# Building a product-key expert layer's gates once, with its activations written out and read back

## The chip, the cores and the metric

The kernel runs on one core of a Trainium2 chip, in one launch. The metric is the time on the device in microseconds (us); the time given for a kernel is the median of its runs.

## What is computed

Two model blocks run on 256 tokens of 1024 features. The change touches one part of the first block, a layer of 128 x 128 = 16384 single-neuron experts from which eight heads choose sixteen each for every token. The chosen pairs of keys come from two searches, and the rest is dense in the kernel: an activation for every expert and token, times a gate that is zero for what was not chosen.

```python
v1, i1 = lax.top_k(s1, PEER_TOPK)            # s1, s2: scores against 128 first and 128 second keys
v2, i2 = lax.top_k(s2, PEER_TOPK)
cand = (v1[..., :, None] + v2[..., None, :]).reshape(T, PEER_HEADS, PEER_TOPK * PEER_TOPK)
vals, ci = lax.top_k(cand, PEER_TOPK)
idx = jnp.take_along_axis(i1, ia, axis=-1) * PEER_NKEYS + jnp.take_along_axis(i2, ib, axis=-1)
gates = jax.nn.softmax(vals, axis=-1)
# for each block of tokens
u = expert_u[ii]
h = jnp.einsum('tkd,td->tk', u, xx).astype(f32)
a = (jax.nn.gelu(h) * gg).astype(x.dtype)
out = jnp.einsum('tk,tkd->td', a, expert_v[ii])
```

## The kernel before, in words

All large products take weights in units of 128 x 1024 fp32. `Emit.run` (L85) walks a list of items in program order; a "w" item is the product of one unit, an "e" item other work. A unit is loaded on SyncE's queue (L96) and split in two parts: ScalarE casts the first, `whi` (L106), VectorE makes the second, `wlo` = raw - whi (L107). There are three buffers of each part, so the split of unit k+3 is written into unit k's buffers. Its instructions are issued right after the product of unit k, and the cast waits until TensorE is through with that product. What an evacuation needs (`em.later`) is issued behind the split.

An expert unit b holds the 128 experts of first key b (the second key is the partition). The layer has two stages of 128 units each:

- **Input products** (`expert_u0`, `expert_e`): 24 matmuls of 128x256 (three for each of 8 chunks, L243 to L245) into one of the four PSUM banks `wk`, which are taken in turn; then GELU on ScalarE. Units 0 to 63 leave their activations in the tile `G0` (128 x 64 x 256 fp32), units 64 to 127 in pairs in DRAM (`uD`, written by GpSimd's queue, L1276). The searches run on VectorE beside units 0 to 63.
- **Output products** (`expert_v`): each unit multiplies one activation, split into `ah` and `al` two units ahead (L374, L375), into four banks `acc` that stay for all 128 units.

The gates are built in groups of 8 tokens by `gbuild(half, g)`, 32 groups for each half of the first keys. `one_hot` makes four tiles on VectorE: `p1` (which pair has which first key, 64 keys), `p2` (the same for the 128 second keys), `ph` and `p1` again (times the high and the low part of the gate). `place` multiplies them on TensorE, 16 matmuls of 128x64 into one `wk` bank (L1248, L1249), which I call a block. For half 0 VectorE multiplies the bank onto `G0` (L1253), among input units 64 to 127; for half 1 ScalarE copies it to `G1` (L1256), among output units 0 to 60. Which unit each step stands before is a table:

```python
gb.setdefault(GB0 + g * GB1 // 31 + 2 * n, []).append(it)         # n = 0 one_hot, n = 1 place
places.setdefault((58 * g + 30) // 31 + 2 * n, []).append(it)
```

So a group's block stands two units behind its one-hots. The second half's activations are read back (L1359) and multiplied with `G1` (L1389, `gated`) in output units 64 to 127.

Of the kernel before, what the change touches and what calls it, by code (L numbers as in the profile page):

```python
# [20 lines left out]
P = 128  # L21
# [27 lines left out]
class Emit:  # L49
    """Items in program order; the weights that they take run ahead of them."""  # L50
# [85 lines left out]
class Halves:  # L136
    """[P, 8, T] in two tiles."""
# [46 lines left out]
def spread(a, b):  # L184
    """Both lists in their orders, evenly among one another."""
# [11 lines left out]
def body(ctx, tc, I, out):  # L197
# [24 lines left out]
    def table(func):  # L222
        """has the engine load a function's table before it is needed."""
# [14 lines left out]
    uD = dram.tile([P, 64, T], F32, name="uD")  # L238
# [21 lines left out]
    def qsum(qs):  # L260
        """four tiles added up, onto the first."""
# [35 lines left out]
    def parts_of(x, gain, y, wk, ready, then=None):  # L297
        """these steps after the last product: the weights' splits come between."""
# [8 lines left out]
    def mm3s(ps, sp, xh, xl, width):  # L307
        """units on the first parts, then on the second ones."""
# [10 lines left out]
    def late_norm(x, r, gain, n, of, when, shift=None, lag=1):  # L319
        """hi + lo = x * r * gain (+ shift) in steps, chunk d in of(d) from the when[d]-th weight item on, or all at once."""  # L320
# [18 lines left out]
    def shift_parts(c0, y):  # L339
        """a shift in two parts behind the tokens."""  # L340
# [9 lines left out]
    def unit_y(ap, y, evac, bank, width=T + 2):  # L350
        """a unit on a norm's input, with a shift's products behind the tokens'."""
# [11 lines left out]
    def npair(pl, tag, width=T):  # L363
        """the pair in npool has room for a shift behind the tokens."""
# [12 lines left out]
    def split_half(src, hi, lo):  # L377
        """of src / 2."""
# [3 lines left out]
    def chunks(o, hi, lo, x, width, order=range(KD)):  # L382
        """a unit's product, chunk of rows by chunk of rows."""
# [6 lines left out]
    def fm(ap, x, evac, bank=bankB):  # L390
        """128 output features on partitions."""
# [6 lines left out]
    def tm(aps, xs, evac, bank):  # L398
        """512 output columns, tokens on partitions; one bank for each (x, token tile)."""
# [24 lines left out]
    class Acc:  # L424
        """1024 output features on partitions, over any number of rows of weights."""
# [16 lines left out]
    def gate_y(pa_, pb_, wk):  # L442
        """in steps: r (x + shift's) of both halves, and silu of the first times the second."""
# [13 lines left out]
    def ffn(w13, w2, y, nx, wk, done, rest, early, ctx=None, mc=None):  # L457
        """items; done(acc) after the last. y holds the norm's input times its gain, and its shift behind the tokens,
        for the first units; rest follows the very first ones and leaves E_["r"], and the norm in nx for the units from
        the early ones on. With ctx, the context's norm: nx holds it behind the tokens, and its activations are left in  # L460
        mc(j)."""
# [11 lines left out]
        def gate(j):  # L473
# [29 lines left out]
            # once the product two before it is through  # L503
# [68 lines left out]
        # the last activations have one product more before they are needed  # L572
# [4 lines left out]
    # ======================= block 1 ========================================  # L577
# [10 lines left out]
    # products of no use keep the array's clock from its idle rate until the first weights are there  # L588
# [3 lines left out]
    # silu(c) of x and the context, on every partition  # L592
# [10 lines left out]
    # constants  # L603
# [4 lines left out]
    # key number, for each of 4 tokens  # L608
# [112 lines left out]
    def decay_logs():  # L721
        """the same of the decays, begun."""
# [4 lines left out]
    def gla_z():  # L727
        # log_sigmoid(z) = min(z, 0) - ln(1 + exp(-|z|))
# [86 lines left out]
    def gla_n():  # L815
        """1/rms of each head's outputs, tokens on partitions: a column for each (head, token tile)."""
# [15 lines left out]
    def gla_r(p):  # L832
        """the same on all partitions: the sums over a diagonal."""
# [99 lines left out]
    # branches: a unit holds two groups of 128 columns, each with 4 chunks of rows  # L933
# [53 lines left out]
    # the branches' steps before these units  # L987
# [10 lines left out]
    # modulation: rows of w_ada^T against silu(c), one output for each partition  # L998
# [20 lines left out]
    # ======================= experts =========================================  # L1019
# [11 lines left out]
    def open_b():  # L1031
        A.close()
        g0 = Gx.enter_context(tc.tile_pool(name="g0", bufs=1))
        B["G", 0] = g0.tile([P, 64, T], F32, name="G0")
        pb = Bx.enter_context(tc.tile_pool(name="pb", bufs=1))
        B["p"] = pb
# [9 lines left out]
    def ctx_norm(name, c0, x, qs, n):  # L1046
        """the context's norm, in steps; x is lost."""
# [40 lines left out]
    def top16(which, width):  # L1088
        """of each (row, values, places), in turn."""
# [17 lines left out]
    # pair (a, b) of a side's ranks comes after all (a' <= a, b' <= b), so (a + 1)(b + 1) <= 16 for a chosen one:  # L1107
    # a = 0 with 16 b, a = 1..3 with 8, a = 4..7 with 4, a = 8..15 with 1, in the order of 16 a + b
# [18 lines left out]
    def pick(t, s_):  # L1127
        """the key that each chosen pair has on side s_, in steps."""
        def a():
# [5 lines left out]
            if s_ == 0:  # L1135
                # a = the number of starts up to the place, less 1: the sum of the keys' steps over them
# [5 lines left out]
            else:  # L1142
                # b = the place & 15, 7, 3, 0 in the four parts
# [30 lines left out]
    def gates(t):  # L1174
        """softmax over each head's pairs, split in two halves; keys and gates to [pair, token]."""
# [41 lines left out]
    def gbuild(half, g):  # L1217
        """gates of all pairs of keys for NG tokens, first keys of one half: [key 2, key 1, token],
        the first half's onto its experts' activations."""
# [3 lines left out]
        def one_hot():  # L1223
            pb = B["pg"]

            def of(t, n):
                """[P, 2, n, 4] of [P, 8]."""
                return t[:, ts].rearrange("p (g t) -> p g t", g=2).unsqueeze(2).to_broadcast([P, 2, n, 4])

            def keys(lo, n):  # L1230
                return iota[:, lo:lo + n, :].unsqueeze(1).to_broadcast([P, 2, n, 4])

            p1 = pb.tile([P, 2, 64, 4], F16, name="p1", tag="p1", bufs=2)
            dve.tensor_tensor(out=p1, in0=keys(half * 64, 64), in1=of(i1T, 64), op=ALU.is_equal)
            p2 = pb.tile([P, 2, P, 4], F16, name="p2", tag="p2", bufs=2)
            dve.tensor_tensor(out=p2, in0=keys(0, P), in1=of(i2T, P), op=ALU.is_equal)
            ph = pb.tile([P, 2, 64, 4], F16, name="ph", tag="ph", bufs=2)
            dve.tensor_tensor(out=ph, in0=p1, in1=of(ghT, 64), op=ALU.mult)
            dve.tensor_tensor(out=p1, in0=p1, in1=of(glT, 64), op=ALU.mult)
            box["t"] = (p2, p1, ph)  # L1240

        def place():
            p2, p1, ph = box.pop("t")
# [6 lines left out]
            ps3 = ps.rearrange("p (t i) -> p t i", t=NG)  # L1250
            o3 = B["G", half][:, :, ts].rearrange("p i t -> p t i")
            if half == 0:
                em.later(lambda: dve.scalar_tensor_tensor(out=o3, in0=ps3, scalar=1.0 / GSCALE, in1=o3,  # L1253
                                                          op0=ALU.mult, op1=ALU.mult))
            else:
# [4 lines left out]
    def open_pg():  # L1260
        B["pg"] = B["p"]
# [854 lines left out]
```

## Time and profile before

| | |
|---|---|
| median of 3 runs (lowest, highest) | 2036.58 us (2035.91, 2038.29) |
| span of the profiled execution | 2036.1 us |
| TensorE matmuls, busy | 2021.8 us (99%) |
| VectorE / ScalarE / GpSimd busy | 1449.1 / 988.5 / 83.9 us |
| chain that ended last, TensorE's share | 94% |

The span reaches from the first instruction to the last. A matmul's record covers its whole passage, and records of neighbours overlap: what one costs is read from the distance between starts in the timeline. Releasers of waits are inferred from semaphores.

### The profile page before, as it was taken

The page shows a single profiled execution, that of the slowest core. Times are in us where ns is not written, and L with a number is a line of the kernel's source. Part 1 is how long each engine was busy: PE and PEld are TensorE (multiplying, and loading weights), DVE is VectorE, ACT ScalarE, POOL GpSimd, SP SyncE. Part 2 cuts the span into 40 slices and gives each one's busy share as a digit, 9 for nine tenths or more (in the row PEclk, how much of TensorE's full clock was granted, in tenths as well). Part 3 has the DMA queues.
Part 4 walks back from the last instruction along what each step waited for, and adds up shares of the span by engine and source line. Part 5 has one row for each costly group of instructions (what it writes and reads, how often), then busy time and mean ns, then how long its engine had stood idle before and what let it go on. Part 6 is the DMA issues. An engine that isn't in the chain of part 4 may idle for free.

```text
span 2036.1 us, 38555 instructions
## 1 busy us (share of the span) xinstructions
PE 2021.8 (99%) x15860; PEld 1941.8 (95%) x15860; DVE 1449.1 (71%) x2410; ACT 988.5 (49%) x1478; POOL 83.9 (4%) x168
## 2 busy tenths in 40 slices
PE   9999999999999999999999999999999999999998
PEld 8899999999999999999998888899989999999998
DVE  7668788877887777789876777578655565568655
ACT  6555545443334555644564333244744455446444
POOL 0000000000000000011000000001000000000000
PEclk9999999999999999999999999999999999999999
DMA  6646555566556556588673666668543333455653
GB/s 243 199 158 192 170 183 182 182 192 194 196 192 209 168 181 197 163 271 280 214 249 115 197 197 205 199 218 297 185 133 106 113 114 112 148 171 174 187 187 124
DMA packets 103952, 376.44 MB, mean 185 GB/s; under 512 B 12055, under 2 KB 12439, under 8 KB 103392
## 3 DMA queue, kind: packets, MB, share of 16 engines
q1 hardware_dynamic: 85968, 310.55, 48.0%
q0 software_dynamic: 16800, 60.74, 9.0%
q8 instruction: 124, 2.03, 0.4%
q10 hardware_dynamic: 1008, 2.70, 0.3%
q14 instruction: 52, 0.43, 0.1%
HBM read 363.45 MB, written 10.49 MB: 184 GB/s over the span
## 4 chain that ended last, share of the span: by engine, by line
PE 94%; DVE 2%; DMA 2%; ACT 1%; issue 0%; SPq 0%; DVEq 0%; ACTq 0%; POOLq 0%
PE wk L243 18%; PE wk L245 18%; PE wk L244 18%; PE acc L243 10%; PE acc L244 10%; PE acc L245 10%; PE acc L414 2%; PE acc L415 2%; PE acc L416 2%; PE wk L1248 2%; PE wk L1249 2%; DVE wlo L107 1%; DMA raw<-pv_dram 1%; DMA raw<-w_dram 1%; ACT whi L106 1%; PE acc L1080 0%
## 5 line engine op out<-in xcount | busy, mean ns | idle before, releaser
L107 DVE TENSOR_TENSOR wlo<-raw,whi 128x1024 fp32r<-128x1024 f32 x587 | 717.3, 1224 | 478.0 <-ACT whi L106 476.2
L106 ACT CAST whi<-raw 128x1024 fp32r<-128x1024 f32 x587 | 615.4, 1049 | 752.8 <-PE wk L244 401.6
L243 PE MATMUL wk<-nhi,whi 128*128 128x256 f32 (+1 forms) x1744 | 495.0, 284 | 0.0
L245 PE MATMUL wk<-nhi,wlo 128*128 128x256 f32 (+1 forms) x1744 | 491.8, 282 | 0.3 <-DVE wlo L107 0.3
L244 PE MATMUL wk<-nlo,whi 128*128 128x256 f32 (+1 forms) x1744 | 490.1, 281 | 0.0
L243 PE MATMUL acc<-ah,whi 128*128 128x256 f32 x1376 | 390.4, 284 | 0.0
L244 PE MATMUL acc<-al,whi 128*128 128x256 f32 x1376 | 388.3, 282 | 0.6 <-DVE al L375 0.4
L245 PE MATMUL acc<-ah,wlo 128*128 128x256 f32 x1376 | 388.1, 282 | 0.0
L244 PEld LDWEIGHTS wk<-nlo,whi 128*128 128x128 f32 x1744 | 329.6, 189 | 0.6 <-issue 0.5
L245 PEld LDWEIGHTS wk<-nhi,wlo 128*128 128x128 f32 x1744 | 329.6, 189 | 0.5 <-DVE wlo L107 0.5
L243 PEld LDWEIGHTS wk<-nhi,whi 128*128 128x128 f32 x1744 | 329.1, 189 | 0.9 <-issue 0.5
L244 PEld LDWEIGHTS acc<-al,whi 128*128 128x128 f32 x1376 | 259.4, 188 | 2.0 <-DVE al L375 1.2
L243 PEld LDWEIGHTS acc<-ah,whi 128*128 128x128 f32 x1376 | 260.1, 189 | 0.9
L245 PEld LDWEIGHTS acc<-ah,wlo 128*128 128x128 f32 x1376 | 259.4, 189 | 0.0
L244 PE MATMUL wk<-nxl,whi 128*128 128x512 f32 (+1 forms) x544 | 188.5, 346 | 0.0
L243 PE MATMUL wk<-nxh,whi 128*128 128x512 f32 (+1 forms) x544 | 188.2, 346 | 0.0
L245 PE MATMUL wk<-nxh,wlo 128*128 128x512 f32 (+1 forms) x544 | 187.4, 344 | 0.0
L374 ACT CAST ah<-G 128x256 fp32r<-128x256 f32 x128 | 52.2, 408 | 177.6 <-PE acc L245 169.6
L245 PEld LDWEIGHTS wk<-nxh,wlo 128*128 128x128 f32 x544 | 102.2, 188 | 13.2
L243 PEld LDWEIGHTS wk<-nxh,whi 128*128 128x128 f32 x544 | 102.1, 188 | 13.0
L244 PEld LDWEIGHTS wk<-nxl,whi 128*128 128x128 f32 x544 | 102.1, 188 | 11.8
L375 DVE TENSOR_TENSOR al<-G,ah 128x256 fp32r<-128x256 f32 x128 | 54.2, 423 | 33.4 <-ACT ah L374 33.1
(536 smaller groups left out, 3312.5 us busy)
## 6 DMA issues: line engine op xcount, KB each, us to landing
raw<-pu_dram SPq DMA_DIRECT2D x128, 512.0 KB, 3.5
raw<-pv_dram SPq DMA_DIRECT2D x128, 512.0 KB, 4.2
row<-ada_dram POOLq DMA_DIRECT2D x59, 512.0 KB, 4.6
raw<-f13a_dram SPq DMA_DIRECT2D x44, 512.0 KB, 3.6
raw<-f2a_dram SPq DMA_DIRECT2D x44, 512.0 KB, 4.5
raw<-f13b_dram SPq DMA_DIRECT2D x44, 512.0 KB, 3.6
raw<-w_dram SPq DMA_DIRECT2D x41, 512.0 KB, 4.2
raw<-f2b_dram SPq DMA_DIRECT2D x22, 512.0 KB, 3.6
```

Source lines behind the costliest of these rows:

```text
L106: nc.scalar.copy(hi, r)
L107: nc.vector.tensor_tensor(out=lo, in0=r, in1=hi, op=ALU.subtract)
L243: pe.matmul(o, whi, xhi, start=start, stop=False)
L244: pe.matmul(o, whi, xlo, start=False, stop=False)
L245: pe.matmul(o, wlo, xhi, start=False, stop=stop)
L374: act.copy(hi, src)
L375: dve.tensor_tensor(out=lo, in0=src, in1=hi, op=ALU.subtract)
L414: pe.matmul(o, xh[:, k, ts], hi[:, sl], start=k == 0, stop=False)
L415: pe.matmul(o, xh[:, k, ts], lo[:, sl], start=False, stop=False)
L416: pe.matmul(o, xl[:, k, ts], hi[:, sl], start=False, stop=k == KD - 1)
L1248: pe.matmul(o, p2[:, g4, :, t4], ph[:, g4, :, t4], start=True, stop=False)
L1249: pe.matmul(o, p2[:, g4, :, t4], p1[:, g4, :, t4], start=False, stop=True)
```

## The change

`gbuild(g)` builds the gates for all 128 first keys at once, in 32 groups. All four tiles have 128 keys x 8 tokens (1024 elements). `place(0)` and `place(1)` take four tokens each: 8 matmuls of 128x128 into a bank of their own, which ScalarE copies to one tile `G` (128 x 128 x 256 fp32). The three steps stand before three consecutive units, all among input units. Every unit's activation goes to DRAM by itself (128 writes of 128 KB in place of 32 of 256 KB; two buffers `act`), and all are read back in pairs (64 reads in place of 32, six ahead after the first), multiplied with `G` (L1384 in the new numbering) and split. The output products have no gate building left. Comments are gone too, so line numbers shift by 2 to 16.

```diff
-TKE, GB0, GB1 = 64, 66, 59
+TKE, GB0, GB1 = 63, 64, 58
+NE = 7
...
-    uD = dram.tile([P, 64, T], F32, name="uD")
+    uD = dram.tile([P, P, T], F32, name="uD")
...
-            p1 = pb.tile([P, 2, 64, 4], F16, name="p1", tag="p1", bufs=2)
-            dve.tensor_tensor(out=p1, in0=keys(half * 64, 64), in1=of(i1T, 64), op=ALU.is_equal)
+            keys = iota.unsqueeze(1).to_broadcast([P, 2, P, 4])
+            p1 = pb.tile([P, 2, P, 4], F16, name="p1", tag="p1", bufs=2)
+            dve.tensor_tensor(out=p1, in0=keys, in1=of(i1T), op=ALU.is_equal)
             p2 = pb.tile([P, 2, P, 4], F16, name="p2", tag="p2", bufs=2)
-            dve.tensor_tensor(out=p2, in0=keys(0, P), in1=of(i2T, P), op=ALU.is_equal)
-            ph = pb.tile([P, 2, 64, 4], F16, name="ph", tag="ph", bufs=2)
-            dve.tensor_tensor(out=ph, in0=p1, in1=of(ghT, 64), op=ALU.mult)
-            dve.tensor_tensor(out=p1, in0=p1, in1=of(glT, 64), op=ALU.mult)
+            dve.tensor_tensor(out=p2, in0=keys, in1=of(i2T), op=ALU.is_equal)
+            ph = pb.tile([P, 2, P, 4], F16, name="ph", tag="ph", bufs=2)
+            dve.tensor_tensor(out=ph, in0=p1, in1=of(ghT), op=ALU.mult)
+            dve.tensor_tensor(out=p1, in0=p1, in1=of(glT), op=ALU.mult)
...
-        def place():
-            p2, p1, ph = box.pop("t")
+        def place(g4):
+            p2, p1, ph = box["t"]
             ps = bankB()
-            for i in range(NG):
-                o = ps[:, i * 64:i * 64 + 64]
-                g4, t4 = i // 4, i % 4
+            for t4 in range(4):
+                o = ps[:, t4 * P:t4 * P + P]
                 pe.matmul(o, p2[:, g4, :, t4], ph[:, g4, :, t4], start=True, stop=False)
                 pe.matmul(o, p2[:, g4, :, t4], p1[:, g4, :, t4], start=False, stop=True)
...
+            em.later(lambda: act.activation(out=o3, in_=ps3, func=AF.Copy, scale=1.0 / GSCALE))
+
+        return ("e", None, one_hot), ("e", None, lambda: place(0)), ("e", None, lambda: place(1))
...
+            u = B["pu"].tile([P, T], F32, name="act", tag="act", bufs=2)
+            act.activation(out=u, in_=ps[:, :T], func=AF.Gelu_apprx_tanh)
+            pool.dma_start(out=uD[:, b, :], in_=u)
...
-        for n, it in enumerate(gbuild(0, g)):
-            gb.setdefault(GB0 + g * GB1 // 31 + 2 * n, []).append(it)
...
+        for n, it in enumerate(gbuild(g)):
+            gb.setdefault(GB0 + g * GB1 // 31 + 1 + n, []).append(it)
+    gb[GB0] = [E(em.flush), E(lambda: open_g())]
+    gb.setdefault(GB0 + GB1 - 4, []).append(E(lambda: load_early(0)))
+    gb[GB0 + GB1 + 3] += [E(em.flush), E(lambda: open_e()), E(lambda: gated(0))]
+    gb[GB0 + GB1 + 4] = [E(lambda: ready1(0)), E(em.flush)]
+    gb[GB0 + GB1 + 5] = [E(lambda: ready1(1))]
...
+    def open_e():
+
+        Cgx.close()
+        B["pe"] = Gx.enter_context(tc.tile_pool(name="pear", bufs=NE - 1))
+        for n in range(1, NE):
+            load_early(n)
...
     def ready1(b):
-        n = b // 2 - 32
+        n = b // 2
         ready(b, C["e", n][:, b % 2, :])
         if b % 2 == 0:
             em.later(lambda: gated(n + 1))
-        elif n + 8 < 32:
-            load_early(n + 8)
+        elif 0 < n and n + NE - 1 < 64:
+            load_early(n + NE - 1)
...
-        for n, it in enumerate(gbuild(1, g)):
-            places.setdefault((58 * g + 30) // 31 + 2 * n, []).append(it)
-    places[60].append(E(lambda: em.later(lambda: gated(0))))
```

How the order moves, at three places. Numbers behind a name tell tiles apart; `whi_5515` and `wlo_5516` are the two parts of one unit.

VectorE and TensorE among the input products, kernel before, around the one-hots `p2_5540`. Each TensorE row stands for a whole unit (24 matmuls) or a whole block (16).

```order
L107 TENSOR_TENSOR wlo_5516<-raw_5513,whi_5515 128x1024
L1234 TENSOR_TENSOR p1_5538<-iota_126,i1T_179 128x512
L1236 TENSOR_TENSOR p2_5540<-iota_126,i2T_180 128x1024
L1238 TENSOR_TENSOR ph_5542<-p1_5538,ghT_181 128x512
L1239 TENSOR_TENSOR p1_5538<-p1_5538,glT_182 128x512
L107 TENSOR_TENSOR wlo_5573<-raw_5570,whi_5572 128x1024
```

```order
L243 MATMUL wk_5488<-nhi_2300,whi_5373 128x256
L1248 MATMUL wk_5521<-ph_5451,p2_5449 128x64
L243 MATMUL wk_5545<-nhi_2300,whi_5423 128x256
L243 MATMUL wk_5579<-nhi_2300,whi_5481 128x256
L1248 MATMUL wk_5612<-ph_5542,p2_5540 128x64
L243 MATMUL wk_5636<-nhi_2300,whi_5515 128x256
```

The one-hots stand on VectorE behind `wlo_5516`, whose unit takes the buffers of the unit `whi_5373`. From the end of that unit to the block that needs `p2_5540`, TensorE has one block and two units.

The same two engines and the same place in the changed kernel, around the one-hots `p2_5748` (blocks of 8 matmuls).

```order
L109 TENSOR_TENSOR wlo_5730<-raw_5727,whi_5729 128x1024
L1231 TENSOR_TENSOR p1_5746<-iota_126,i1T_179 128x1024
L1233 TENSOR_TENSOR p2_5748<-iota_126,i2T_180 128x1024
L1235 TENSOR_TENSOR ph_5750<-p1_5746,ghT_181 128x1024
L1236 TENSOR_TENSOR p1_5746<-p1_5746,glT_182 128x1024
L109 TENSOR_TENSOR wlo_5781<-raw_5778,whi_5780 128x1024
```

```order
L245 MATMUL wk_5702<-nhi_2300,whi_5590 128x256
L1244 MATMUL wk_5737<-ph_5655,p2_5653 128x128
L245 MATMUL wk_5753<-nhi_2300,whi_5634 128x256
L1244 MATMUL wk_5788<-ph_5750,p2_5748 128x128
L245 MATMUL wk_5797<-nhi_2300,whi_5685 128x256
L1244 MATMUL wk_5832<-ph_5750,p2_5748 128x128
L245 MATMUL wk_5848<-nhi_2300,whi_5729 128x256
```

Here `wlo_5730` takes the buffers of the unit `whi_5590`. From the end of that unit to the first block that needs `p2_5748`, TensorE has one half block and one unit.

TensorE and ScalarE in the changed kernel where two groups follow each other without a free unit, which happens four times: `g * 58 // 31` then grows by 1 and not by 2. `G_5359` is the tile `G`, the banks are `wk`.

```order
L1244 MATMUL wk_6073<-ph_6035,p2_6033 128x128
L245 MATMUL wk_6089<-nhi_2300,whi_5970 128x256
L1244 MATMUL wk_6124<-ph_6035,p2_6033 128x128
L1244 MATMUL wk_6133<-ph_6086,p2_6084 128x128
L245 MATMUL wk_6142<-nhi_2300,whi_6014 128x256
L1244 MATMUL wk_6178<-ph_6086,p2_6084 128x128
L245 MATMUL wk_6194<-nhi_2300,whi_6065 128x256
```

```order
L108 CAST whi_6116<-raw_6114 128x1024
L1249 ACTIVATE G_5359<-wk_6073 128x4x128
L1257 ACTIVATE act_6121<-wk_6089 128x256
L108 CAST whi_6169<-raw_6167 128x1024
L1249 ACTIVATE G_5359<-wk_6124 128x4x128
L1249 ACTIVATE G_5359<-wk_6133 128x4x128
L1257 ACTIVATE act_6175<-wk_6142 128x256
```

With four banks in turn, the unit `wk_6142` takes the bank of `wk_6073`, and `wk_6194` that of `wk_6124`. Each of these is emptied behind a cast.

## Rows read from the trace of the kernel before

**Rows 1.** Page, the span and the engines' busy time.

```profile
span 2036.1 us, 38555 instructions
PE 2021.8 (99%) x15860; PEld 1941.8 (95%) x15860; DVE 1449.1 (71%) x2410; ACT 988.5 (49%) x1478; POOL 83.9 (4%) x168
```

**Rows 2.** Busy time by stage: input units 0-63, 64-127, output units 0-62.

```profile
core 0: us, PE busy (x) PEld busy (x) DVE busy (x) ACT busy (x) POOL busy (x), PEclk, DMA share, GB/s
250.00:433.00 183.00, 183.00 (x1543) 183.00 (x1543) 152.01 (x477) 90.62 (x136) 0.00 (x0) 1.00 0.59 183
440.00:647.80 207.80, 207.80 (x1974) 206.51 (x1974) 165.75 (x214) 82.04 (x124) 16.19 (x30) 1.00 0.60 195
647.80:860.80 213.00, 213.00 (x2023) 211.58 (x2022) 157.28 (x255) 121.31 (x161) 8.00 (x15) 1.00 0.58 182
```

**Rows 3.** Groups of instructions by line, 647.8 to 860.8 us (output units).

```profile
L1256 ACT ACTIVATE G<-wk 128x512 f32<-128x512 f32 x32 | 35.8, 1119 | 0.0
L1249 PE MATMUL wk<-p,p 128*128 128x64 f16 x256 | 35.3, 241 | 0.0
```

**Rows 4.** Timeline of TensorE, two units and two blocks, input units 64-127: start us, length.

```profile
526.16 0.28 PE L245 MATMUL wk<-nhi,wlo 128*128 128x256 f32 x1
526.28 0.23 PE L1248 MATMUL wk<-ph,p 128*128 128x64 f16 x1
...
532.92 0.28 PE L245 MATMUL wk<-nhi,wlo 128*128 128x256 f32 x1
533.04 0.23 PE L1248 MATMUL wk<-ph,p 128*128 128x64 f16 x1
...
533.95 0.24 PE L1249 MATMUL wk<-p,p 128*128 128x64 f16 x1
534.00 0.36 PE L243 MATMUL wk<-nhi,whi 128*128 128x256 f32 x1
534.20 0.28 PE L244 MATMUL wk<-nlo,whi 128*128 128x256 f32 x1
```

**Rows 5.** Timeline of TensorE, matmuls of 512 columns.

```profile
36.58 0.39 PE L415 MATMUL acc<-wlo,nhi 128*128 128x512 f32 x1
36.81 0.39 PE L416 MATMUL acc<-whi,nlo 128*128 128x512 f32 x1
```

**Rows 6.** Timelines of ScalarE and VectorE, the same two units as rows 4.

```profile
526.36 1.06 ACT L106 CAST whi<-raw 128x1024 fp32r<-128x1024 f32 x1 [1.52 <-PE wk L244]
527.32 0.39 ACT L1274 ACTIVATE scr<-wk 128x256 f32<-128x256 f32 x1
```

```profile
527.46 1.23 DVE L107 TENSOR_TENSOR wlo<-raw,whi 128x1024 fp32r<-128x1024 f32 x1 [0.36 <-ACT whi L106]
528.60 0.42 DVE L1234 TENSOR_TENSOR p<-iota,i1T 128x512 f16<-128x512 f16 x1
528.94 0.68 DVE L1236 TENSOR_TENSOR p<-iota,i2T 128x1024 f16<-128x1024 f16 x1
529.54 0.41 DVE L1238 TENSOR_TENSOR ph<-p,ghT 128x512 f16<-128x512 f16 x1
529.99 0.42 DVE L1239 TENSOR_TENSOR p<-p,glT 128x512 f16<-128x512 f16 x1
```

**Rows 7.** Waits of ScalarE and VectorE, 440 to 648 us: total us, times, longest.

```profile
ACT whi L106 <- PE wk L244: 124.5, 60, 2.6
...
DVE wlo L107 <- ACT whi L106: 40.5, 55, 2.7
```

**Rows 8.** DMA to and from `uD`: the products, and landing times of writes, then reads.

```profile
L1389 DVE TENSOR_TENSOR G<-G,G x32: 681/684/690, 861.1 to 1037.3; 128x512 f32<-128x512 f32 x32
```

```profile
DMA to landing us min/median/max: 2.3/2.5/5.1
```

```profile
DMA to landing us min/median/max: 2.8/4.6/8.0
```

**Rows 9.** TensorE's longest early wait, and the granted clock around it.

```profile
8.92 0.38 PE L919 MATMUL acc<-yah,whi 128*128 128x256 f32 x1 [1.34 <-ACT whi L106]
...
8.00:12.00 4.00, 3.02 (x21) 2.66 (x22) 3.55 (x8) 4.00 (x7) 0.00 (x0) 1.00 0.69 241
```

More of the change, by code (lines that the diff above doesn't have):

```diff
@@ L1032, in open_b @@
         A.close()
[L1033 to L1034 removed]
         pb = Bx.enter_context(tc.tile_pool(name="pb", bufs=1))
[L1036 removed]
+        B["p"] = B["pu"] = pb
         for s_ in range(2):
@@ L1215, in body, with gbuild @@
     NG = 8
-    def gbuild(half, g):
+    def gbuild(g):
         ts = slice(g * NG, g * NG + NG)
@@ L1223, in one_hot, with of @@
         def one_hot():
[L1224 to L1231, printed above, removed]
-            p1 = pb.tile([P, 2, 64, 4], F16, name="p1", tag="p1", bufs=2)
-            dve.tensor_tensor(out=p1, in0=keys(half * 64, 64), in1=of(i1T, 64), op=ALU.is_equal)
+            pb = B["p"]
+            def of(t):
+                return t[:, ts].rearrange("p (g t) -> p g t", g=2).unsqueeze(2).to_broadcast([P, 2, P, 4])
@@ L1252, in place @@
[L1252 to L1255, printed above, removed]
-                em.later(lambda: act.activation(out=o3, in_=ps3, func=AF.Copy, scale=1.0 / GSCALE))
-        return ("e", None, one_hot), ("e", None, place)
-    def open_pg():
-        B["pg"] = B["p"]
-    def expert_u0(b):
-        def ev(ps):
-            act.activation(out=B["G", 0][:, b, :], in_=ps[:, :T], func=AF.Gelu_apprx_tanh)
-        return fm(I["pu"][b], X2, ev)
@@ L1269, in expert_e @@
-    def expert_e(b):
-        def ev(ps):
-            if b % 2 == 0:
-                B["early"] = scr(B["p"], (P, 2, T))
-            act.activation(out=B["early"][:, b % 2, :], in_=ps[:, :T], func=AF.Gelu_apprx_tanh)
-            if b % 2 == 1:
-                pool.dma_start(out=uD[:, b - 65:b - 63, :], in_=B["early"])
+            ps3 = ps.rearrange("p (t i) -> p t i", t=4)
+            t0 = g * NG + 4 * g4
+            o3 = B["G"][:, :, t0:t0 + 4].rearrange("p i t -> p t i")
+            em.later(lambda: act.activation(out=o3, in_=ps3, func=AF.Copy, scale=1.0 / GSCALE))
@@ L1310, in body @@
     items += [("w", list(I["wq"][0:2]), first_units)] + [early_q(j) for j in range(2, NQ - 1)]
-    items += [("e", None, em.flush), ("e", None, open_b), ("e", None, open_pg), ("e", None, lambda: first_q(range(4)))]
+    items += [("e", None, em.flush), ("e", None, open_b), ("e", None, lambda: first_q(range(4)))]
     items += [early_q(NQ - 1), ("e", None, lambda: first_q([4]))]
@@ L1328, in body @@
         tk += pick(t, 0) + ga_[:1] + pick(t, 1) + ga_[1:]
-    ub = [expert_u0(b) for b in range(64)]
+    ub = [expert_u(b) for b in range(P)]
     ub[1:1] = [score(15)]
     ub[0:0] = [score(14)]
-    ub += [expert_e(b) for b in range(64, P)]
     gb = {}
     for g in range(T // NG):
-        for n, it in enumerate(gbuild(0, g)):
-            gb.setdefault(GB0 + g * GB1 // 31 + 2 * n, []).append(it)
-    for b in range(2):
-        gb[GB0 + GB1 + 3 + b] = [E(lambda b=b: ready(b, B["G", 0][:, b, :]))]
+        for n, it in enumerate(gbuild(g)):
[5 more added lines that the diff above has]
+    gb[GB0 + GB1 + 5] = [E(lambda: ready1(1))]
     items += over(ub, gb, TKE, tk)
@@ L1342, in body, with open_g @@
     Cgx = ExitStack()
-    def open_c():
+    def open_g():
         Bx.close()
-        g1 = Gx.enter_context(tc.tile_pool(name="g1", bufs=1))
-        B["G", 1] = g1.tile([P, 64, T], F32, name="G1")
-        B["pg"] = Cgx.enter_context(tc.tile_pool(name="pg", bufs=1))
+        g = Gx.enter_context(tc.tile_pool(name="g", bufs=1))
+        B["G"] = g.tile([P, P, T], F32, name="G")
+        B["pu"] = Gx.enter_context(tc.tile_pool(name="pu", bufs=1))
+        C["e", 0] = B["pu"].tile([P, 2, T], F32, name="early0")
+        B["p"] = Cgx.enter_context(tc.tile_pool(name="pg", bufs=1))
+    def open_e():
[3 more added lines that the diff above has]
+            load_early(n)
     def part(a, n):
-        return B["G", 0][:, a:a + n, :]
+        return B["G"][:, a:a + n, :]
     def flat(t):
@@ L1357, in load_early @@
     def load_early(n):
-        C["e", n] = part(2 * (n % 8), 2)
+        if n > 0:
+            C["e", n] = B["pe"].tile([P, 2, T], F32, name="early", tag="early")
         pool.dma_start(out=C["e", n], in_=uD[:, 2 * n:2 * n + 2, :])
@@ L1382, in ready1 @@
             em.later(lambda: gated(n + 1))
-        elif n + 8 < 32:
-            load_early(n + 8)
+        elif 0 < n and n + NE - 1 < 64:
+            load_early(n + NE - 1)
     def gated(n):
-        if n < 32:
-            dve.tensor_tensor(out=C["e", n], in0=C["e", n], in1=B["G", 1][:, 2 * n:2 * n + 2, :], op=ALU.mult)
+        if n < 64:
+            dve.tensor_tensor(out=C["e", n], in0=C["e", n], in1=part(2 * n, 2), op=ALU.mult)
     def expert_v(b):
@@ L1479, in body @@
     first = []
-    places = {}
-    for g in range(T // NG):
-        for n, it in enumerate(gbuild(1, g)):
-            places.setdefault((58 * g + 30) // 31 + 2 * n, []).append(it)
-    places[60].append(E(lambda: em.later(lambda: gated(0))))
-    loads = {36: lambda: load_early(0), 38: lambda: load_early(1), 40: lambda: load_early(2),
-             42: lambda: load_early(3), 44: lambda: load_cs(pool, 0), 46: lambda: load_cs(pool, 1), 48: lambda: load_early(4),
-             50: lambda: load_early(5), 52: lambda: load_ctx(0), 54: lambda: load_ctx(1), 55: silu_cs,
-             56: lambda: load_early(6), 58: lambda: load_early(7), 60: load_rows}
+    loads = {44: lambda: load_cs(pool, 0), 46: lambda: load_cs(pool, 1), 52: lambda: load_ctx(0),
+             54: lambda: load_ctx(1), 55: silu_cs, 60: load_rows}
     for b in range(64):
@@ L1492, in body @@
         first += [ev(b)]
-        first += places.get(b, [])
         if b in loads:
@@ L1506, in body @@
         lambda: em.later(lambda: ncc([0, 1, 2, 3, 4, 5, 6, 7])))]
-    items += [("e", None, open_c)] + first + [("e", None, Cgx.close)]
+    items += first
     for i, u in enumerate(second):
```

5 lines of the change are left out of this document (1 added, 4 removed).

## The prediction

> **What bounds the kernel now.** I read the page's busy times first, then the busy time by stage, then the timelines of a few units, then the waits. TensorE is busy for 99% of the 2036.1 us [rows 1], and in the three expert stages that the change touches it has no gap at all: 183.0 of 183.0, 207.8 of 207.8 and 213.0 of 213.0 us, at full clock [rows 2]. So every microsecond of matmul that goes there shortens the run, and every wait that appears there lengthens it. VectorE is busy for 80% of the middle stage and ScalarE for 39% [rows 2]; they have time left, but not at any moment: the cast of a unit's weights waits for TensorE to end the unit three before (60 waits, 124.5 us) and the second part waits for the cast (55 waits, 40.5 us) [rows 7]. VectorE takes its instructions in order, so whatever stands behind that second part on its queue starts only then.
>
> One unit and one block are priced by starts. From block to block there are two units: 526.28 to 533.04, 6.76 us. The block's sixteen matmuls start 0.061 us apart (533.04 to 533.95 is fifteen steps); from its first start to the second matmul of the next unit are 1.16 us, of which 0.12 is that unit's own first step (526.16 to 526.28) [rows 4]. So a block costs 1.04 us, 0.97 of it matmuls and 0.07 the change from one kind to the other, and a unit (6.76 - 1.04) / 2 = 2.86 us.
>
> **The change, part by part.**
>
> *Output products.* 32 blocks go, 512 matmuls in all (256 on each of two lines, [rows 3]): 32 x 1.04 = **-33.3 us**, all on the path, since TensorE is busy throughout. VectorE's one-hots and ScalarE's copies go there too, at no gain.
>
> *Input products, matmuls.* 32 blocks of sixteen 64-column matmuls become 64 half blocks of eight 128-column ones. No row shows a 128-column fp16 matmul. At 64 columns the step is 0.061 us; at 256 columns 0.12 [rows 4], and at 512 columns 0.23 [rows 5]. Those two differ by 0.11 for 256 columns, which led back to 128 columns gives 0.06 and at 64 would give 0.04: the 64-column step is already above the columns' own time. So I take 0.061, the end nearest to that line, and keep 0.118 as the other. A half block is 8 x 0.061 + 0.07 = 0.56 us; 64 x 0.56 - 33.3 = **+2.5 us**. The Trainium skill, "TensorE: Matmul & The Clock Gate", section "Back-to-back issue gap", gives about 81 ns as the sustained step of weight load and matmul at 128 columns; by it the sum below would be about 2059 us. The rows are nearer, so they stand.
>
> *Input products, the one-hots.* Now they have time to spare: the unit ends at 526.28 (where the block starts), the cast starts at 526.36, the second part at 527.46, the one-hots at 528.60, and the last ends at 529.99 + 0.42 = 530.41; the block wants them at 533.04 [rows 4, 6]. The margin is 2.63 us. The change takes from it three times. The first half block stands one unit sooner: 2.86. What stands ahead of the unit in between is half a block: 1.04 - 0.56 = 0.48. And the one-hots are longer: now 528.60 to 530.41, 1.81 us; then the two comparisons at 0.60 each (as 528.94 to 529.54), and the two dependent products at 0.45 and 0.42 [rows 6] plus 0.26 each for 512 elements more (0.68 - 0.42), 2.61 us in all: 0.80. The margin becomes 2.63 - 2.86 - 0.48 - 0.80 = -1.51 us. TensorE waits 1.5 us at a group's first half block. (The first of the eight matmuls needs only three of the tiles and goes ahead, 0.06; the signal takes about 0.08, as from 526.28 to 526.36. They cancel.) Nothing makes up for the wait: the next group's one-hots hang by the same chain on a unit that was itself late, so it recurs. While TensorE waits the other engines run dry too, so nothing is late behind them: second parts and casts have a whole unit to spare.
>
> The groups with this wait: of 32, the four that follow another without a free unit have their one-hots in time, and so has the group behind each (below). 24 x 1.5 = 36.0; the first of them has no half block ahead, 0.6 more: **+36.6 us**.
>
> *Input products, banks.* Units and half blocks alternate in four banks, so each bank comes round after two units, which ScalarE can meet: cast 1.06, copy 1.12, GELU 0.39 [rows 3, 6] are 2.6 of 3.4 us. At the four places with two half blocks in a row a unit comes round to a bank whose copy stands behind a cast that waits for the unit just ended: 0.08 + 1.06 + 1.12 = 2.26 us after it, against two half blocks of work (1.12), a wait of 1.15; and at the next unit 2.26 against one half block (0.56), 1.7. After that the next one-hots are in time. 4 x 2.85 = **+11.4 us**.
>
> *Writes and reads.* In input units each activation is written alone. The buffer is wanted again two units on, 5.7 us; GELU 0.39, some 0.3 to the issue and 2.5 us to land (5.1 at worst) [rows 6, 8] stay below or at it. SyncE's weight loads are untouched. The reads of output units 0 to 63 are new: 32 more, landing in 4.6 us (8.0 at worst) [rows 8], ordered six pairs ahead (twelve units, 34 us); VectorE's product of 0.68 us a pair [rows 8] lies beside a unit's 1.23 for the second part, in the place of the one-hots. All at nothing; if the first reads land at the worst, some 2 us once.
>
> *Sum.* -33.3 + 2.5 + 36.6 + 11.4 = +17.2. Against the profiled 2036.1 us that is 2053.3, and as the median of the runs stands 0.5 above that span, **2054 us**.
>
> **Bounds of the forecast.** If the 128-column step is 0.118, only half of it shows (the second half block runs while TensorE would wait anyway): 256 x 0.057 = 14.6, 2068 us. If the dependent products follow at 0.60 like the others, 24 x 0.2 = 5 less, and if the four bank waits don't come, 11.4 less: 2038 with both, 2042 with the larger alone.
>
> **The rivals.**
>
> 1. *The waits don't come: faster.* VectorE would have to be through with the one-hots 3.4 us after the unit's end (0.56 + 2.86) and not 4.9. For it: VectorE is idle for a fifth of the stage, and if the one-hots did not stand behind a second part that waits for TensorE, they would be done a unit earlier. Against it: the order shows them behind it, and rows 7 show that wait in nearly every unit. Then the matmuls' saving stays: 2036.6 - 33.3 + 2.5 + 11.4 = 2017 us. It decides from a chain under 3.4 us on. Chance 0.10.
> 2. *128-column matmuls are dear.* The fp16 operands are read with a step of four elements, and 0.061 for 64 columns may hide a slow read that doubles. 2068 us as above. Against it: the three widths line up. Chance 0.10.
> 3. *The writes become the bound.* If a write took the 8.0 us that the slowest read took, GELU would wait for its buffer, and with it the casts behind it on ScalarE: 8.7 against 5.7 us for two units, 3.0 x 32 = 96 us in input units 0 to 63: 2150 us. Against it: no write took over 5.1. Chance 0.03.
> 4. *The clock falls in the waits.* At 1.2 GHz the 58 units of the stage would take 2.86 us more each, 166, and the 48 of the waits would vanish in them: 2172 us. Against it: a wait of 1.34 us stands in a stretch with the granted clock at 1.00, its 2.4 GHz level [rows 9]. Chance 0.03.
> 5. *It cancels.* Waits a little over half as long, with the saving as it is, leave the time where it was, about 2037. Chance 0.04.
>
> **How the numbers follow.** The forecast has 0.70. With rival 2 that is 0.80 between 2042 and 2068, which is the range; the rest lies outside on both sides. About 0.2% (4 us) is what a measurement of this kernel tells from no change. Faster: rival 1, 0.10. Same: rival 5, 0.04. Slower: the forecast and rivals 2 to 4, 0.70 + 0.10 + 0.03 + 0.03 = 0.86.
>
> **What would show it.** Right: the output units 0 to 63 take 64 x 2.86 = 183 us; in the input units 64 to 127 TensorE waits some 24 times about 1.5 us for VectorE's one-hots and some eight times 1 to 2 us for ScalarE's copies, and two units with a group take about 8.3 us instead of 6.76; the granted clock stays. Wrong: no such waits on TensorE, a 128-column step well above 0.06, output units with waits for the reads, or gaps in input units 0 to 63.

## The result, and the profile after

The changed kernel takes 2064.47 us (median of 4 runs, 2063.85 to 2068.38), the kernel before 2036.82 us on the same chip (2035.91 to 2038.29): 1.0137 times as long, 95% interval [1.0123, 1.0151]. The page of the profiled execution begins so, to be set beside [rows 1]:

```profile
span 2062.2 us, 37798 instructions
PE 2024.5 (98%) x15348; PEld 1934.7 (94%) x15348; DVE 1399.5 (68%) x2282; ACT 1017.5 (49%) x1510; POOL 153.5 (7%) x296
```

The span is 26.1 us longer, with 512 matmuls fewer and yet 2.7 us more of TensorE's busy time. Where the time went is read by stage, in the windows that answer to [rows 2] (input units 0 to 63, the rest of the input stage, output units 0 to 63; the same columns):

```profile
250.00:433.00 183.00, 181.52 (x1527) 181.18 (x1526) 153.43 (x476) 90.22 (x136) 34.39 (x64) 1.00 0.71 229
440.00:707.00 267.00, 245.73 (x1994) 233.71 (x1993) 152.48 (x186) 142.85 (x189) 37.09 (x70) 1.00 0.53 160
707.00:890.00 183.00, 183.00 (x1545) 183.00 (x1543) 122.32 (x158) 90.48 (x132) 20.70 (x39) 1.00 0.77 246
```

The output products now start at 707.13 us; before, they started at 647.79. So the input stage is 59.3 us longer, and what follows it 33.2 us shorter (1355.1 us to the end of the span in place of 1388.3). The last window is the gain: 64 output units in 183 us without a gap, 2.86 each. The middle one is the loss: TensorE, which had no gap there before, is now idle for 21.3 of 267 us. The waits of TensorE, 440 to 710 us, name the causes (total us, times, longest):

```profile
PE wk L1245 <- DVE p L1236: 10.0, 23, 0.4
PE wk L1244 <- DVE ph L1235: 6.7, 23, 0.3
...
PE wk L245 <- ACT G L1249: 4.2, 4, 1.1
```

So 23 groups wait for VectorE's products twice, and four units wait for ScalarE's copy of a bank, one at each of the four places with two half blocks in a row (called doubles below). A 24th group, the first, waits at 432.47 us; the trace puts its first wait (1.24 us) down to ScalarE's GELU, but `ph` ended there at 432.41, 0.06 us ahead of the matmul, as in the other groups. The idle time that is recorded before an instruction is less than what the wait costs, since a matmul's record outlasts the distance between starts; by starts, a group's two waits are 1.05 us. The timeline of TensorE shows both, at a first half block that waits and at a second one that doesn't:

```profile
520.55 0.28 PE L247 MATMUL wk<-nhi,wlo 128*128 128x256 f32 x1
521.12 0.29 PE L1244 MATMUL wk<-ph,p 128*128 128x128 f16 x1 [0.29 <-DVE ph L1235]
521.85 0.28 PE L1245 MATMUL wk<-p,p 128*128 128x128 f16 x1 [0.43 <-DVE p L1236]
521.94 0.30 PE L1244 MATMUL wk<-ph,p 128*128 128x128 f16 x1
...
522.54 0.29 PE L1245 MATMUL wk<-p,p 128*128 128x128 f16 x1
522.58 0.37 PE L245 MATMUL wk<-nhi,whi 128*128 128x256 f32 x1
...
525.39 0.28 PE L247 MATMUL wk<-nhi,wlo 128*128 128x256 f32 x1
525.51 0.29 PE L1244 MATMUL wk<-ph,p 128*128 128x128 f16 x1
...
526.33 0.30 PE L1245 MATMUL wk<-p,p 128*128 128x128 f16 x1
526.38 0.37 PE L245 MATMUL wk<-nhi,whi 128*128 128x256 f32 x1
```

Where nothing is waited for, the seven steps from 525.51 to 526.33 take 0.82 us: **0.118 us for each 128-column step**, not the 0.061 of the sum. From first start to first start a half block takes 0.87 us here, and 1.46 where it waits; the unit before it takes 2.93 in the one case (522.58 to 525.51) and 3.39 in the other. The difference is the wait, 0.59 + 0.46 = 1.05. A unit and a half block without a wait are 2.93 + 0.87 = 3.80, so with 2.86 for the unit a half block costs 0.94.

The chain that makes the wait is as the prediction drew it. VectorE, around the same one-hots:

```profile
518.03 1.22 DVE L109 TENSOR_TENSOR wlo<-raw,whi 128x1024 fp32r<-128x1024 f32 x1 [3.62 <-ACT whi L108]
519.18 0.68 DVE L1231 TENSOR_TENSOR p<-iota,i1T 128x1024 f16<-128x1024 f16 x1
519.78 0.68 DVE L1233 TENSOR_TENSOR p<-iota,i2T 128x1024 f16<-128x1024 f16 x1
520.38 0.69 DVE L1235 TENSOR_TENSOR ph<-p,ghT 128x1024 f16<-128x1024 f16 x1
521.10 0.69 DVE L1236 TENSOR_TENSOR p<-p,glT 128x1024 f16<-128x1024 f16 x1
521.83 1.23 DVE L109 TENSOR_TENSOR wlo<-raw,whi 128x1024 fp32r<-128x1024 f32 x1
```

and ScalarE ahead of it, whose cast had waited for the unit that ends at 516.87 (the start of the half block behind it):

```profile
516.95 1.06 ACT L108 CAST whi<-raw 128x1024 fp32r<-128x1024 f32 x1 [2.56 <-PE wk L246]
```

From the unit's end, by way of the cast, the second part and the four one-hots, to the matmul that needs the last of them (521.85) are 4.98 us. The order leaves one half block and one unit for it, 3.80, and that matmul's own step of 0.12: it is 1.06 us late.

### The profile page after: what moved, and what is told of

Its sections match the earlier page's. It is cut to its first block, busy times and chain, and to the rows that moved or that the text cites. A ratio compares the mean times of both kernels' runs of the same rounds, so it can differ in the third digit from the quotient of the medians.

```text
span 2062.2 us, 37798 instructions
## 1 busy us (share of the span) xinstructions
PE 2024.5 (98%) x15348; PEld 1934.7 (94%) x15348; DVE 1399.5 (68%) x2282; ACT 1017.5 (49%) x1510; POOL 153.5 (7%) x296
## 4 chain that ended last, share of the span: by engine, by line
PE 90%; DVE 6%; ACT 2%; DMA 1%; issue 1%; ACTq 0%; DVEq 0%; POOLq 0%
PE wk L245 17%; PE wk L246 17%; PE wk L247 16%; PE acc L246 10%; PE acc L247 10%; PE acc L245 10%; PE acc L416 2%; PE acc L417 2%; PE acc L418 2%; DVE wlo L109 2%; ACT whi L108 2%; PE wk L1245 1%; DVE p L1236 1%; DVE ph L1235 1%; DVE p L1231 1%; DVE p L1233 1%
## 5 line engine op out<-in xcount | busy, mean ns | idle before, releaser
L376 ACT CAST ah<-early 128x256 fp32r<-128x256 f32 x128 | 52.2, 408 | 167.6 <-PE acc L247 162.7
L1258 POOL DMA_DIRECT2D uD<-act x128 | 69.4, 542 | 443.5 <-ACT act L1257 369.8
```

What stands on the lines that cost most here:

```text
L376: act.copy(hi, src)
L1258: pool.dma_start(out=uD[:, b, :], in_=u)
```

## The experiments

Ten kernels were run beside the changed one, and the changed kernel itself once more. The step is the distance between starts of a half block's matmuls (of a block's, in the last two rows), which have 128 columns (64); where the first step of a block differs, it is read from the second matmul on. Each ratio is to runs of the kernel before on the same chip.

| kernel | median us | ratio to the kernel before | 95% interval | step, us |
|---|---|---|---|---|
| changed kernel | 2064.47 | 1.0137 | [1.0123, 1.0151] | 0.118 |
| moving operands side by side | 2054.83 | 1.0082 | [1.0065, 1.0099] | 0.057 |
| weights side by side | 2064.40 | 1.0137 | [1.0120, 1.0154] | 0.117 |
| moving operands, step of eight | 2097.10 | 1.0301 | [1.0284, 1.0318] | 0.230 |
| two tokens side by side | 2054.25 | 1.0084 | [1.0067, 1.0101] | 0.058 |
| half blocks a unit later | 2039.60 | 1.0010 | [1.0001, 1.0020] | 0.117 |
| a unit later, other banks | 2031.23 | 0.9970 | [0.9958, 0.9982] | 0.118 |
| two tokens, a unit later | 2018.33 | 0.9907 | [0.9892, 0.9922] | 0.059 |
| two tokens, a unit later, other banks | 2002.23 | 0.9827 | [0.9813, 0.9840] | 0.058 |
| before, moving operands side by side (64 columns) | 2011.98 | 0.9874 | [0.9859, 0.9889] | 0.034 |
| before, two tokens side by side (64 columns) | 2009.33 | 0.9855 | [0.9837, 0.9873] | 0.031 |

### What the 128-column step is made of

The matmul operands (`p2`, `ph`, `p1`) are slices of tiles in which four tokens lie side by side, so a matmul takes every fourth fp16 element. Three runs change that step for the moving operands or for the weights. In the first, `flat` takes 128 neighbouring elements.

```diff
-                pe.matmul(o, p2[:, g4, :, t4], ph[:, g4, :, t4], start=True, stop=False)
-                pe.matmul(o, p2[:, g4, :, t4], p1[:, g4, :, t4], start=False, stop=True)
+                pe.matmul(o, p2[:, g4, :, t4], flat(ph), start=True, stop=False)
+                pe.matmul(o, p2[:, g4, :, t4], flat(p1), start=False, stop=True)
```

> The changed kernel, but the half blocks read their moving operands (the two gate tiles) as 128 elements that lie side by side, not with a step of four elements; the elements read are others, so the gates are wrong, and nothing else is left out. Theory S (the step of four elements halves the rate at which TensorE takes the moving operand): the distance between starts falls from 0.118 to about 0.06 us, a half block from 0.96 to 0.56, TensorE's wait for the one-hots grows back from 1.03 to about 1.5 us, and the time is 2052 to 2054 us, the forecast. Theory C (128 columns of fp16 cost 0.118 however they lie): step, waits and time stay, 2064 us. Theory W (the weights, read with the same step, set the distance): the same as C.

The second half block that waits for nothing, in this kernel:

```profile
523.42 0.25 PE L1245 MATMUL wk<-ph,p 128*128 128x128 f16 x1
523.50 0.22 PE L1246 MATMUL wk<-p,p 128*128 128x128 f16 x1
...
523.84 0.22 PE L1246 MATMUL wk<-p,p 128*128 128x128 f16 x1
523.87 0.36 PE L245 MATMUL wk<-nhi,whi 128*128 128x256 f32 x1
```

Six steps in 0.34 us, 0.057 each; a half block is 0.45 us from first start to first start. The time is 2054.83, just above the 2052 to 2054 that theory S gave, and the wait per group is back at 1.5 (a group's first half block takes 1.08 us, its unit 3.80). The converse, with the weights alone side by side:

```diff
-                pe.matmul(o, p2[:, g4, :, t4], ph[:, g4, :, t4], start=True, stop=False)
+                pe.matmul(o, flat(p2), ph[:, g4, :, t4], start=True, stop=False)
```

(and the same for `p1`).

> The changed kernel, but the half blocks read their stationary operand (the one-hots of the second keys) side by side, and the moving ones as before with a step of four elements; the gates are wrong, nothing else is left out. Theory W: the distance between starts falls to about 0.06 us and the time to 2052 to 2054. Theories S and C: nothing changes, 0.118 us and 2064.

2064.40 us, step 0.117: nothing changed. Theory W falls, and with the run above so does C. The third run goes the other way, a step of eight, where `s8` takes every eighth element (it was made last of all, with the results of the next sections known):

```diff
-                pe.matmul(o, p2[:, g4, :, t4], ph[:, g4, :, t4], start=True, stop=False)
+                pe.matmul(o, p2[:, g4, :, t4], s8(ph), start=True, stop=False)
```

> The changed kernel with the moving operands of the half blocks read with a step of eight elements (16 bytes); the gates are wrong, nothing else is left out. So far: 0.057 us for 128 elements side by side, 0.058 with a step of two, 0.118 with four. If the price goes on with the bytes passed over: about 0.236 us a step, a half block 0.94 us longer; that length also lets the one-hots catch up, so the 24 waits of 1.05 and the waits at the four doubles shrink to little, and the time is 2064.5 + 60 - 25 - 6 = about 2093 us. If any step above two elements costs the same: 0.118 and 2064.

```profile
502.72 0.40 PE L1245 MATMUL wk<-ph,p 128*128 128x128 f16 x1
502.94 0.41 PE L1246 MATMUL wk<-p,p 128*128 128x128 f16 x1
...
506.17 0.41 PE L1246 MATMUL wk<-p,p 128*128 128x128 f16 x1
```

Fifteen steps in 3.45 us, 0.230: twice the price of a step of four, as the bytes passed over. The time, 2097.10, lies 4 us above what was expected; 2.8 us of it are two units at a lower clock, each behind a double half block (last section).

### The same computation with a step of two

One layout computes the gates unchanged and halves the step: four groups of two tokens instead of two of four.

```diff
-            p1 = pb.tile([P, 2, P, 4], F16, name="p1", tag="p1", bufs=2)
+            p1 = pb.tile([P, 4, P, 2], F16, name="p1", tag="p1", bufs=2)
...
-                pe.matmul(o, p2[:, g4, :, t4], ph[:, g4, :, t4], start=True, stop=False)
+                pe.matmul(o, p2[:, 2 * g4 + t4 // 2, :, t4 % 2], ph[:, 2 * g4 + t4 // 2, :, t4 % 2], start=True, stop=False)
```

> The changed kernel with the one-hot tiles laid out for two tokens side by side instead of four (four groups of 128 keys x 2 tokens), so that the matmuls read both operands with a step of two elements. Theory S with a rate that follows the bytes passed over: the distance between starts falls from 0.118 to about 0.06 us, time 2052 to 2054. Theory C: 0.118 and 2064. A third case: VectorE's one-hots get longer with pieces of two elements (0.7 us each now); each 0.1 us on each of the four adds 0.4 to every one of the 24 waits, 10 us in all.

2054.25 us, and 0.058 for the step (six from the second matmul to the last, 0.35 us); VectorE's four one-hots stay at 0.68 to 0.69 us. A half block that waits for nothing:

```profile
521.67 0.23 PE L1244 MATMUL wk<-ph,p 128*128 128x128 f16 x1
521.74 0.22 PE L1245 MATMUL wk<-p,p 128*128 128x128 f16 x1
...
522.09 0.22 PE L1245 MATMUL wk<-p,p 128*128 128x128 f16 x1
522.12 0.36 PE L245 MATMUL wk<-nhi,whi 128*128 128x256 f32 x1
```

The gates are those of the changed kernel, so it was not the other values in the run with operands side by side that made that one fast. This kernel is the prediction's own case, with the step that it took, and so shows whether the rest of the sum was right. Its waits, 440 to 710 us:

```profile
PE wk L1244 <- DVE ph L1235: 16.8, 23, 0.7
PE wk L1245 <- DVE p L1236: 11.3, 23, 0.5
PE wk L245 <- ACT G L1249: 9.2, 7, 1.5
```

By starts a group waits 0.88 us on its unit (3.80 for 2.92) and 0.65 in its half block (1.10 for 0.45): 1.53, where the prediction had 1.51. At the double half blocks a unit waits 1.25 us and the next 1.70; the prediction had 1.15 and 1.7.

### The waits

The two half blocks one unit later (three and four units after the table's start for a group, instead of two and three), the rest as changed:

```diff
-            gb.setdefault(GB0 + g * GB1 // 31 + 1 + n, []).append(it)
+            gb.setdefault(GB0 + g * 57 // 31 + 1 + n + (n > 0), []).append(it)
```

> The changed kernel, but both half blocks stand one unit later behind their one-hots, and the groups are spread over 57 units instead of 58. Theory A (the wait is the distance: the one-hots are 1.0 us late because the half block stands only one unit behind them): TensorE's 24 waits for VectorE go, 24.7 us and 1 for the first group, and some five bank waits of about 1.2 us stay: 2037 to 2041 us, level with the kernel before. Rival B (VectorE as a whole is too slow for one group in two units, so the lateness returns at any distance): the waits come back after the first few groups and the time stays above 2058.

2039.60 us: every wait for the one-hots is gone, and five units wait for a copy (5.2 us recorded), one at each of the five doubles that 57 units leave. Rival B falls: VectorE has the time, it is only asked too soon. What five bank waits cost is read from the starts, at a double half block and the single one behind the next unit:

```profile
486.04 0.29 PE L1245 MATMUL wk<-p,p 128*128 128x128 f16 x1
486.46 0.39 PE L245 MATMUL wk<-nhi,whi 128*128 128x256 f32 x1
...
490.23 0.29 PE L1245 MATMUL wk<-p,p 128*128 128x128 f16 x1
491.56 0.39 PE L245 MATMUL wk<-nhi,whi 128*128 128x256 f32 x1 [1.04 <-ACT G L1249]
```

Elsewhere a unit starts 0.04 to 0.05 us after the half block's last matmul. Here it is 0.42 and 1.33, so a double costs 0.37 + 1.29 = 1.66 us, of which the list of waits has only the larger. The next run takes the banks from the other pool:

```diff
             p2, p1, ph = box["t"]
-            ps = bankB()
+            ps = bankA()
```

> The kernel with the half blocks one unit later, and these take banks of the other pool (the one that output products use) instead of the units' four. Theory A (what is left there is five bank waits of about 1.2 us each): they go, 2039.6 - 6 = 2033 to 2035 us. The working leads to the same place: 2037.5 for the kernel before, - 33.3 + 28.1 = 2032.3. Rival (the waits move to the other pool's banks, or the copies get later): 2039 us or more.

2031.23 us, 8.4 less than the run before: five doubles of 1.66 are 8.3. I had expected 6, by the recorded waits alone. At a double half block the next unit now starts 0.05 us behind it, and TensorE's list of waits holds none in this stage:

```profile
525.60 0.29 PE L1245 MATMUL acc<-p,p 128*128 128x128 f16 x1
525.65 0.37 PE L245 MATMUL wk<-nhi,whi 128*128 128x256 f32 x1
```

### Together

Two runs put these edits together: two tokens side by side and the half blocks a unit later, and then the other pool's banks as well.

> The changed kernel with both: tiles with two tokens side by side, and the half blocks one unit later. If both findings add: 2039.6 - 64 x 0.46 = 2010, but the five places with two half blocks in a row then have only 1.0 us of matmuls in place of 1.9 and bank waits of about 2.9 us as the prediction had them, in place of 1.2: + 5 x 1.7 = 8, so 2016 to 2020 us. If the shorter half blocks bring the one-hot waits back at this distance too: above 2025.

2018.33 us, within the range. The half blocks are short again, so the waits at the doubles are long again: the list has ten, where it had five for the half blocks a unit later alone.

```profile
PE wk L245 <- ACT G L1249: 12.8, 10, 1.5
```

> All three: two tokens side by side, one unit later, banks of the other pool. With no wait left the sum is 2037.5 - 33.3 + 64 x (0.50 + 0.02) for the half blocks, that is 2006 to 2008 us, the fastest of all. If a wait on the other pool's banks or a one-hot wait is left, each of 1 us a group adds 24 to 32: 2030 or more.

```profile
span 2001.1 us, 37792 instructions
```

2002.23 us, the fastest of all, 4 us under the expected 2006 to 2008. The sum as it was written does not lead to that range: 2037.5 - 33.3 + 64 x 0.52 is 2037.5, since it leaves out the input stage's own 32 blocks, another 33.3 us. With them it is 2004.2. A half block from first start to first start measures 0.44 to 0.45, and with the change of kind around it 0.50, where 0.52 had been put in: 2037.5 - 66.6 + 64 x 0.50 = 2002.9, within 1 us of the time.

### What the 64-column step was

The prediction had read 0.061 us at 64 columns as a floor. The next two runs take the kernel before and change its operands as above: the moving ones side by side, and then the layout with two tokens, which leaves the computation as it is.

> The kernel before (64-column matmuls), with the moving operands read as 64 elements side by side; its gates are wrong, nothing else is left out. What it tells: what the 0.061 us of the step at 64 columns was. Theory S alone (the slow read is all of it, 64 elements at 0.92 ns): the step falls well below, to about 0.03, and the kernel gains up to 1024 x 0.03 = 31 us: 2006. Theory F (another floor of about 0.055 to 0.06, which a 128-column matmul with operands side by side shows as well, hid the slow read): the step stays at 0.055 to 0.061, time 2031 to 2037.5.

> The kernel before with its one-hot tiles laid out for two tokens side by side, everything else as it was. Theory S: the 64-column step falls from 0.061 to about 0.034 us as with operands side by side, and the kernel gains the same 25 us: 2011 to 2013. Theory C or a price for any step above one: it stays at or near 2037. Besides it tells what the rebuilt gates are worth once the slow read is gone on both sides: 2002.2 against this time.

Of the kernel before with operands side by side, from the second matmul of a block on:

```profile
526.67 0.20 PE L1250 MATMUL wk<-p,p 128*128 128x64 f16 x1
526.70 0.20 PE L1249 MATMUL wk<-ph,p 128*128 128x64 f16 x1
...
527.14 0.20 PE L1250 MATMUL wk<-p,p 128*128 128x64 f16 x1
```

Fourteen steps in 0.47 us, 0.034, and the time is 2011.98 us: 25 less, where theory S had up to 31. With two tokens side by side, again from the second matmul on:

```profile
525.47 0.20 PE L1249 MATMUL wk<-p,p 128*128 128x64 f16 x1
...
525.90 0.19 PE L1249 MATMUL wk<-p,p 128*128 128x64 f16 x1
```

Fourteen steps in 0.43 us, 0.031, and the kernel before takes 2009.33 us, 28 less (2 us below what was expected). So 0.061 was the slow read as well, and theory F falls: 64 elements with a step of four take 0.061, 128 of them 0.118.

What the rebuilt gates are worth once both sides read well and nothing waits is less certain. The ratios are 0.9827 (with the later half blocks and the other banks besides) and 0.9855 for the kernel before, some 6 us, but the intervals overlap a little. By starts, a block of the kernel before with two tokens side by side costs 0.56 us (0.49, and 0.07 for the change of kind) and a half block 0.50, which is 4 us on 64.

The changed kernel was timed once more beside the kernel before with two tokens side by side.

> The changed kernel as it is, beside the run above on the same chip: 2064 us, for the ratios of the experiments.

2065.52 us, 1.0137 [1.0118, 1.0155], the same as the first time.

## Why the prediction was right, and which term was not

The forecast was 2054 us in a range of 2042 to 2068, slower with 0.86. The kernel is slower and in the range, 10 us above the forecast; almost all of the difference is one price. By the terms:

| term, us | predicted | measured | how |
|---|---|---|---|
| output products, 32 blocks go | -33.3 | -33.2 | start of the output stage to the end of the span |
| 64 half blocks for 32 blocks | +2.5 | +26.5 | 64 x 0.935 - 33.3 |
| waits for one-hots | +36.6 | +26.3 | 23 x 1.055, and 2.0 at the first group |
| waits for banks, four doubles | +11.4 | +6.6 | 4 x (0.37 + 1.29) |
| sum | +17.2 | +26.2 | spans: +26.1 |

**The step that failed is the price of the 128-column matmul.** The prediction led two widths back to 128 columns and took the 64-column step, 0.061, for a floor "above the columns' own time". But the widths that it compared were not alike: the matmuls of 256 and 512 columns read fp32 operands that lie side by side [rows 4, 5], those of 64 read every fourth fp16 element. The runs give 0.034 at 64 columns and 0.057 at 128 with operands side by side, and 0.061 and 0.118 with the step of four. A row that stands above a line of others is a sign that something else sets it, and here that something grew with the columns. Rival 2 named the mechanism and gave 2068 us; it had a chance of 0.10 because "the three widths line up", and that was the wrong reading. Of the signs of being wrong that the prediction names, this one came, "a 128-column step well above 0.06".

**The two wait terms were right as mechanisms and wrong in size only through that step.** In the layout with a step of two, where the price is what the forecast had taken, they measure 1.53 us a group and 1.25 + 1.70 a double, against 1.51 and 1.15 + 1.7, and the time is 2054.25 against 2054. In the changed kernel the longer half block hides part of them: it runs while the one-hots are still being made and while the copies empty the banks. The 2068 us for this price had let it shorten the waits for the one-hots, but had kept the bank waits at 11.4 us; 6.6 were measured. So 0.057 us on 512 matmuls, which is 29 us, cost only 10 us.

**The rivals.** The waits came (rival 1 not), in all the 24 groups that were forecast. The writes did not become the bound (rival 3): the page has them landing after 3.8 us in the median, where 2.5 had been put in, GELU waited for a buffer three times, 5.0 us in all, and input units 0 to 63 have no gap but the first group's wait at 432.47 us. The clock stayed at 1.00 in the whole stage, its 2.4 GHz level, through 24 groups of waits (rival 4); the windows above show it. Nothing cancelled (rival 5). The reads in output units 0 to 63 are hidden, as forecast: TensorE has no gap in their 183 us.

The sustained step of about 81 ns at 128 columns, which the prediction cited from the Trainium skill, "TensorE: Matmul & The Clock Gate", section "Back-to-back issue gap", is met by no run here: 0.057 us with operands side by side and 0.118 with a step of four lie on either side of it.

## What to carry over

Price a matmul from a row with the same width, type and layout, and when a short one stands above the line of wider ones, ask what it reads before calling it a floor. When work is merged, look at how far it now stands behind its producer: two units of distance had been ample and one was 1 us short in 24 of 32 groups, which cost 26 of the 33 us that the output products had saved; one unit more gave 25 us back. A price and a wait are not independent terms of a sum, since dearer work ahead of a wait shortens it.

## What the runs showed of the hardware

In these runs TensorE's time for the moving operand follows the bytes that it passes over once the step is above two fp16 elements: 128 elements take 0.057 us side by side, 0.058 with a step of two (4 bytes), 0.118 with four (8 bytes) and 0.230 with eight (16 bytes). Only fp16 was tried, so a rule that counts elements and not bytes would fit as well. The step of the weights does little: 0.117 us with them side by side against 0.118 with a step of four. The Trainium skill, "Advanced Engine Details and Errata", section "SBUF Cachelines", says that at least two accesses to a 16-byte line are needed to absorb the latency. A step of 8 bytes makes two, and the runs show it at half rate, so for this operand two were not enough, while four (the step of two) cost nothing.

In the run with a step of eight the granted clock fell at the end of two of the four double half blocks. The windows of that kernel, before, at and after one (same columns as rows 2):

```profile
494.00:502.70 8.70, 8.70 (x62) 7.35 (x60) 7.22 (x10) 3.92 (x6) 1.08 (x2) 1.00 0.44 113
502.70:506.20 3.50, 3.50 (x18) 1.83 (x17) 1.45 (x2) 2.27 (x3) 0.54 (x1) 0.95 0.52 147
506.20:508.50 2.30, 2.30 (x12) 2.30 (x11) 0.00 (x0) 0.00 (x0) 0.00 (x0) 0.50 0.70 242
```

After sixteen matmuls at 0.230 us, with TensorE busy throughout by its records, the clock stood at 0.50, its 1.2 GHz level, and the next unit took 4.31 us; behind a second of the four doubles it took 4.57, behind the other two 3.06 and 3.04. The first two units are together 2.8 us longer than the other two, of the 4 us that this run lies above its expectation. In the changed kernel, with gaps of 0.29 and 0.43 us by the records in 24 groups, the clock stayed at 1.00. So the clock fell in a stretch of slow reads and not in one with short waits; that it was the read and not something else at that place was not tried by itself.
